# Output projection scalings dealt over the second product, weight tiles swapped, stores of combined down weights two steps later

## The chip, the cores and the metric

The kernel runs on one core of one Trainium2 chip. The core's engines are TensorE (PE, with its weight loads shown as PEld), VectorE (DVE), ScalarE (ACT), GpSimd (POOL) and SyncE (SP), which here issues the DMAs. The metric is device time in microseconds, the median of several executions.

## The reference

One decoder layer over 2048 rows of width 1024, all in float32. The parts that matter here are these:

```python
o_hg = rmsnorm(o_hg, hg_out_norm) * silu(hg)             # (T, 512)
o_sb = rmsnorm(stick_breaking_mix(sq, sk, sv), sb_out_norm)   # (T, 512)
mix = jnp.concatenate([o_hg, o_sb], axis=-1) @ w_out     # output projection
h = h + rmsnorm(mix, attn_post_norm)
u = rmsnorm(h, ffn_pre_norm)
gate, up = jnp.split(u @ w_gate_up, [D_FF], axis=-1)     # D_FF = 2816
y = (silu(gate) * up) @ w_down
h = h + rmsnorm(y, ffn_post_norm)
h = h + (p @ ple_proj) * sigmoid(h @ ple_gate)
```

## The kernel before

**Products.** The 2048 rows are worked on in four groups of 512. A float32 matrix product is made of three matmuls, from operands that are split into a high and a low half (`mm3`, L221 to L223). ACT casts the high half; DVE or POOL subtracts it from the source, which gives the low half (L207/L208, L845/L846 and L1073/L1074 in the profile). In the tile names `uh`/`ul` and `wh`/`wl` are such halves.

From group 2 on, two groups are taken together, and each pair of 2x2 block matrices is multiplied in seven products instead of eight, in the order `CHAIN = (1, 2, 6, 3, 7, 5, 4)`. The operands of some products are sums and differences of blocks (L1086, L1089); the results are added into `cu`, `c11`, `c12` and so on as each product ends (`chain`, also L1086/L1089).

**The joint output projection.** `out_pair(2)` projects groups 2 and 3. Position `pos` is 0 to 6, `prod` its product. Each product has four tiles `i` of twelve matmuls: four blocks `k`, three matmuls each. `w_prep(pos, k)` brings the weights: they come from `w_out` as `wr` and are split, or come from `wo_p` already split. `a_prep` brings the left operand. While tiles 0 and 1 of a position run, the weights of the next position are prepared, two blocks at each.

The left operand has a half that belongs to the stick-breaking group (`raws[4..7]`, in tiles named `wl` and `wh`), whose rows must be scaled by a factor that is not known earlier. `over_rows` spreads the factor over a tile (four transposes at L792 and a copy by ACT to `acc`, L794). `scaled` multiplies by it and by the gain `g_sb` (L798). The scaled blocks are then added to `s2`, and the sums are split as the left operand of product 6. All of this is written ahead of the last tile (i = 3) of product 1. Beside the products run the rest of the previous groups' work (`post_mix`, L930 to L955) and the first operands of gate_up.

**The down weights.** In the first gate_up (`gate_up(0)`, 77 steps, a step being one product of a block, two tiles), hooks run after given steps. At steps 36, 40, ... 76, `down_combos(k)` loads four blocks of `w_down` into `wr` buffers (`load`, L1058), combines them on DVE (`b_combos`, L1086) and stores the four results to `wd_s[k]` (L1104), which `down` reads later. Other hooks in these steps read rows of `h_s`, scale them on ACT (L992), transpose them on TensorE (`turner`: tile `hg`, L1006) and store them to `u_s` (L1012). The 12 `wr` buffers of that pool (`WR = 12`) also carry the weights of gate_up.

**Order.** TensorE's order is the written one. The order on DVE, ACT, POOL and SP comes from a simulation of the program's time; instructions under `pin` keep the written order among themselves.

Of the kernel before, what the change touches and what calls it, by code (L numbers as in the profile page):

```python
# [13 lines left out]
ALU = mybir.AluOpType  # L14

P = 128
# [3 lines left out]
GT = 512  # L20
NG = T // GT
TT = GT // P
HH = 4
SBH = 8
SBD = 64
DFF = 2816
# [64 lines left out]
def hybrid_block(  # L91
# [6 lines left out]
    nc = tc.nc  # L98
    ctx.enter_context(tc.manual_schedule(engines={mybir.EngineType.PE}))
    x, p, out = x[0], p[0, 0], out[0]  # L100
    w_in, w_out, w_gate_up, w_down = w_in[0], w_out[0], w_gate_up[0], w_down[0]
# [67 lines left out]
    def bank(tag):  # L169
        return ps.tile([P, 512], F32, tag=tag, name=tag, bufs=BANKS[tag])  # L170
# [4 lines left out]
    def mm_bank():  # L175
        mm_count[0] += 1
        return bank(mm_tags[mm_count[0] % len(mm_tags)])
# [25 lines left out]
    pin = tc.keep_in_program_order  # L203
# [21 lines left out]
    def cut(pair, j):  # L225
        return pair[0][:, j * P:(j + 1) * P], pair[1][:, j * P:(j + 1) * P]
# [58 lines left out]
    def operand(pool, tag, bufs):  # L285
        return [pool.tile([P, GT], F32R, tag=tag + s, name=tag + s, bufs=bufs) for s in ("h", "l")]
# [502 lines left out]
    def over_rows(rr, tag, new):  # L789
        b = bank(tag)  # L790
        for t in range(TT):
            nc.tensor.transpose(b[:, t * P:(t + 1) * P], rr[:, t:t + 1].to_broadcast((P, P)), ident)  # L792
        e = new()
        nc.scalar.copy(e, b)  # L794
        return e

    def scaled(k, raw, r):
        nc.vector.scalar_tensor_tensor(raw, raw, g_sb[:, k:k + 1], r, op0=ALU.mult, op1=ALU.mult)  # L798

    def first_rows(g, tt):  # L800
        acc = ev(name="oss")
# [21 lines left out]
    def out_pair(g, tt, rr):  # L823
        sw = {}
        cs = [{} for _ in range(TT)]
        raws, s2 = {}, {}

        def w_prep(pos, k):
            prod = CHAIN[pos]
            if pos % 2:  # L830
                hi, lo = slot("wh", 0, "wh", F32R), slot("wl", 0, "wl", F32R)
            else:
                hi, lo = operand(wpool, "u", UB)
            sw[prod, k] = hi, lo
            if prod in (6, 3, 7):
                for n, t in enumerate((hi, lo)):
                    nc.sync.dma_start(t.bitcast(F32), wo_p[k][KEPT[prod], n])
                return
            raw = wpool.tile([P, GT], F32, tag="wr", name="wr", bufs=4)
            if prod in (1, 2):  # L840
                r = (HH * (prod - 1) + k) * P
                nc.sync.dma_start(raw, w_out[r:r + P, 0:GT])
            else:
                nc.sync.dma_start(raw, wo_s[k][0 if prod == 5 else 1])
            nc.scalar.copy(hi, raw)  # L845
            (V if k % 2 else G).tensor_tensor(lo, raw, hi.bitcast(F32), op=ALU.subtract)  # L846

        def a_prep(pos, k):
            prod = CHAIN[pos]
            if prod == 3:  # L850
                a12 = load(on_s[k])
                sub(V, s2[k], a12, s2[k])
                t, e = s2[k], V
            elif prod == 7:
                t = load(o_s[g][k])
                sub(V, t, t, raws[k])
                e = V
            elif prod == 5:
                t = raws[k]
                add(V, t, t, raws[HH + k])  # L860
                e = V
            else:
                t, e = raws[HH + k], V
            tt[prod, k] = split(wpool, "u", UB, t, e)

        def rows(half, j, i):
            m = cs[i][1 + half, 1 + j]
            nc.sync.dma_start(h2_s[g + half][i * P:(i + 1) * P, j * GT:(j + 1) * GT], m)
            nc.scalar.activation(junk, m, AF.Square, scale=ROOT, accum_out=sums_m[half][:, 2 * i + j:2 * i + j + 1])

        def before(pos, i):
            if (pos, i) == (0, 3):
                r = over_rows(rr, "tr", new_acc)
                for k in range(HH):
                    scaled(k, raws[HH + k], r)
                    add(V, s2[k], s2[k], raws[HH + k])
                    tt[6, k] = split(wpool, "u", UB, s2[k], V)

        def new_acc():
            return slot("acc", 0, "acc")  # L880

        for k in range(HH):
            w_prep(0, k)
        for i in range(ND):
            if i in (2, 3):
                raws[i] = slot("wr", 0, "wr")
            else:
                tag = "wh" if i % 2 else "wl"
                raws[i] = wpool.tile([P, GT], F32, tag=tag, name=tag, bufs=3)
            nc.sync.dma_start(raws[i], o_s[g + 1][i])  # L890
        for k in range(HH):
            s2[k] = load(o_s[g][k])
            sub(V, s2[k], raws[k], s2[k])
        for k in range(HH):
            w_prep(1, k)
        for pos, prod in enumerate(CHAIN):
            for i in range(TT):
                before(pos, i)
                b = mm_bank()
                for k in range(HH):  # L900
                    mm3(b, cut(tt[prod, k], i), sw[prod, k], k == 0, k == HH - 1)
                chain(prod, cs[i], b, new_dn)
                if prod == 2:
                    rows(0, 0, i)
                elif prod == 5:
                    rows(0, 1, i)
                    rows(1, 1, i)
                elif prod == 4:
                    rows(1, 0, i)
                if 1 <= pos < len(CHAIN) - 1 and i < 2:  # L910
                    for k in (2 * i, 2 * i + 1):
                        w_prep(pos + 1, k)
                        if pos > 1:
                            a_prep(pos + 1, k)
                yield
            if prod in (5, 4):
                half = 0 if prod == 5 else 1
                r, x = row_scales[:, half, 0:TT], hgss[:, g + half, :]
                pair = sums_m[half].rearrange("p (t j) -> p t j", j=2)
                nc.gpsimd.tensor_tensor(r, pair[:, :, 0], pair[:, :, 1], op=ALU.add)  # L920
                for _ in range(2):
                    nc.gpsimd.tensor_tensor(r, r, x, op=ALU.mult)
                nc.gpsimd.tensor_scalar(r, r, EPS, None, op0=ALU.add)
                nc.gpsimd.tensor_tensor(r, r, neghalf.to_broadcast((P, TT)), op=ALU.pow)
                nc.gpsimd.tensor_tensor(r, r, x, op=ALU.mult)
# [126 lines left out]
    def slot(tag, side, name, dt=F32):  # L1052
        side = side if big[side] is not None else 0
        return big[side].tile([P, GT], dt, tag=f"{tag}{side}", name=name, bufs=SLOTS[tag.rstrip("hl")][side])

    def load(src, shape=None):
        r = slot("wr", 0, "wr")
        nc.sync.dma_start(r if shape is None else shape(r), src)  # L1058
        return r
# [25 lines left out]
    def sub(e, o, a, b):  # L1085
        return e.tensor_tensor(o, a, b, op=ALU.subtract)  # L1086

    def add(e, o, a, b):
        return e.tensor_tensor(o, a, b, op=ALU.add)  # L1089

    V, G = nc.vector, nc.gpsimd

    def b_combos(b11, b12, b21, b22, e):

        sub(e, b11, b12, b11)
        sub(e, b12, b22, b12)
        sub(e, b22, b22, b11)
        sub(e, b21, b22, b21)

    def combos(blk, dst, e):  # L1100
        t = [load(blk(i, j)) for i, j in ((0, 0), (0, 1), (1, 0), (1, 1))]
        b_combos(*t, e)
        for i, r in zip((1, 3, 4, 2), t):
            nc.sync.dma_start(dst[i - 1], r)  # L1104

    wd_s = [dram.tile([4, P, GT], F32, tag=f"wd_s{k}", name=f"wd_s{k}") for k in range(DFF // 256)]
    wp_s = [dram.tile([4, P, GT], F32, tag=f"wp_s{k}", name=f"wp_s{k}") for k in range(ND // 2)]

    def down_combos(k):
        def blk(i, j):  # L1110
            r = (2 * k + i) * P
            return w_down[r:r + P, j * GT:(j + 1) * GT]

        combos(blk, wd_s[k], V)

    def ple_combos(k):
        def blk(i, j):
# [354 lines left out]
    g_sb = column("g_sb", sb_out_norm[0], HH, later)  # L1472
# [121 lines left out]
    def at(stage, step, f):  # L1594
        hooks.setdefault((stage, step), []).append(f)

    def spread(stage, step, gen, n, every=1):
        st = Stream(gen)
        for i in range(n):
            at(stage, step + i * every, st.step)  # L1600
# [4 lines left out]
    def turner(src, dst, gain, scales=None):  # L1605
        return turn(src, dst, gain, ["hg"], wr, acc, scales)
# [4 lines left out]
    spread(0, 19, post_late(NG - 1), 2 * TT, 4)  # L1611
    for k in range(DFF // 256):
        at(0, 36 + 4 * k, lambda k=k: down_combos(k))
    spread(0, 34, turner(h_s[2], u_s[2], g_ffn, rows_h[0]), 10, 2)
    spread(0, 54, turner(h_s[3], u_s[3], g_ffn, rows_h[1]), 10, 2)
    spread(2, 59, make_pt(), 9, 2)
# [42 lines left out]
```

## Time and profile before

| | |
|---|---|
| median of 3 runs | 2965.28 us (2963.56 to 2966.44) |
| the profiled execution | 2966.78 us, its span 2965.0 us, granted clock 0.992 |
| TensorE busy | 97% of the span, 17796 matmuls |
| DVE / ACT / POOL busy | 71% / 53% / 47% |
| DMA | 635.27 MB, queue 1 busy 67.5% of 16 engines' span |

In rows of the profile a line names time and duration (us), engine, source line, operation, `output<-input` and the tile's shape. In brackets stands how long the engine was idle before it, and what released it. Rows `SPq` are DMA issues. A wait in a list is given as engine, tile and line, who released it, then the sum in us, how often, and the longest.

### The profile page before, as it was taken

How to read it: one execution, taken by the hardware profiler on the slowest of the kernel's cores; microseconds unless marked ns; L12 is line 12 of the kernel's file. 1: busy time of each engine (PE TensorE's matmuls, PEld its weight loads, DVE VectorE, ACT ScalarE, POOL GpSimd, SP SyncE). 2: the span in 40 equal slices, each digit the busy share in tenths (PEclk: the TensorE clock that was granted, in tenths of full speed). 3: DMA queues.
4: the chain of work that ended last, by engine and by line, in shares of the span. 5: the costliest groups of instructions: out<-in, count | busy, mean ns of one | idle time of the engine just before them, and what ended most of it. 6: DMA issues, size and time to landing. Idle time of an engine off the chain costs nothing. (4 is left out here: it accounts for less than half of the span.)

```text
span 2965.0 us, 51986 instructions
## 1 busy us (share of the span) xinstructions
PE 2862.4 (97%) x17796; PEld 2397.8 (81%) x17796; DVE 2114.2 (71%) x3051; ACT 1581.2 (53%) x3220; POOL 1387.7 (47%) x1384
## 2 busy tenths in 40 slices
PE   9999999999999999988999999999999999999999
PEld 7878888877888788877788778788888888888777
DVE  4776777777788777756977777756877765666685
ACT  5667657666667666765623333455433233545542
POOL 3345456545665666764433211355722121456653
PEclk9999999999999999999999999999999999999999
DMA  7785576456556454448986787867965555677975
GB/s 230 234 257 169 173 222 207 143 168 211 182 184 183 147 155 131 142 146 310 331 283 211 253 275 265 269 204 226 325 217 174 177 172 174 214 221 236 329 253 168
DMA packets 487561, 635.27 MB, mean 214 GB/s; under 512 B 45184, under 2 KB 275584, under 8 KB 487296
## 3 DMA queue, kind: packets, MB, share of 16 engines
q1 hardware_dynamic: 487296, 631.95, 67.5%
q8 instruction: 141, 2.31, 0.3%
q14 instruction: 124, 1.02, 0.1%
HBM read 459.29 MB, written 172.49 MB: 213 GB/s over the span
## 5 line engine op out<-in xcount | busy, mean ns | idle before, releaser
L1073 ACT CAST wh<-wr 128x512 fp32r<-128x512 f32 x592 | 347.1, 618 | 501.0 <-PE mm L222 110.5
L1074 POOL TENSOR_TENSOR wl<-wr,wh 128x512 fp32r<-128x512 f32 x256 | 370.2, 1454 | 439.8 <-ACT wh L1073 390.6
L452 POOL TENSOR_TENSOR a<-be,ring 128x512 f32<-128x512 f32 (+2 forms) x320 | 325.5, 1018 | 410.0 <-DVE ring L448 382.9
L1074 DVE TENSOR_TENSOR wl<-wr,wh 128x512 fp32r<-128x512 f32 x336 | 303.4, 911 | 159.4 <-ACT wh L1073 136.4
L221 PE MATMUL mm<-uh,wh 128*128 128x512 f32 x968 | 401.4, 415 | 7.9 <-DVE vv L365 4.4
L223 PE MATMUL mm<-uh,wl 128*128 128x512 f32 x968 | 380.5, 393 | 0.0
L222 PE MATMUL mm<-ul,wh 128*128 128x512 f32 x968 | 380.2, 393 | 0.0
L448 DVE TENSOR_TENSOR_SCAN ring<-z,ring,be 128x512 f32<-128x512 f32 x192 | 245.6, 1279 | 88.2 <-ACT z L434 83.5
L221 PE MATMUL mm<-wh,uh 128*128 128x256 f32 (+1 forms) x840 | 262.4, 312 | 2.9 <-DVE eb L351 2.2
L222 PE MATMUL mm<-wl,uh 128*128 128x256 f32 (+1 forms) x840 | 249.4, 297 | 4.1 <-POOL wl L208 2.6
L223 PE MATMUL mm<-wh,ul 128*128 128x256 f32 (+1 forms) x840 | 248.7, 296 | 0.0
L433 ACT ACTIVATE be<-z 128x512 f32<-128x512 f32 (+2 forms) x320 | 171.1, 535 | 100.6 <-DVE z L431 60.9
L465 DVE TENSOR_TENSOR al<-tr,ah 128x512 fp32r<-128x512 f32 (+1 forms) x320 | 191.6, 599 | 43.7 <-ACT ah L463 42.1
L221 PEld LDWEIGHTS mm<-uh,wh 128*128 128x128 f32 x968 | 183.5, 190 | 43.4 <-issue 3.8
L223 PEld LDWEIGHTS mm<-uh,wl 128*128 128x128 f32 x968 | 182.5, 189 | 41.2
L207 ACT CAST wh<-wr 128x512 fp32r<-128x512 f32 x256 | 158.6, 619 | 102.4 <-PE mm L222 51.1
L463 ACT CAST ah<-tr 128x512 fp32r<-128x512 f32 (+1 forms) x320 | 167.8, 524 | 84.6 <-PE tr L460 83.0
L208 POOL TENSOR_TENSOR wl<-wr,wh 128x512 fp32r<-128x512 f32 x128 | 171.5, 1340 | 78.8 <-ACT wh L207 58.7
L222 PEld LDWEIGHTS mm<-ul,wh 128*128 128x128 f32 x968 | 183.4, 190 | 30.4
L460 PE MATMUL tr<-ident,a 128*128 128x128 f32 x1088 | 178.4, 276 | 19.5 <-POOL a L452 19.5
L427 PE MATMUL z<-kt,q 128*128 128x512 f32 (+3 forms) x640 | 189.4, 377 | 0.0
L1074 POOL TENSOR_TENSOR wl<-s,wh 128x512 fp32r<-128x512 f32 x40 | 62.2, 1557 | 269.8 <-ACT wh L1073 224.9
(387 smaller groups left out, 7598.3 us busy)
## 6 DMA issues: line engine op xcount, KB each, us to landing
wr<-in_w_gate_up_dram SPq DMA_DIRECT2D x292, 256.0 KB, 4.3
wr<-in_w_in_dram SPq DMA_DIRECT2D x224, 256.0 KB, 3.3
wr<-hid_s SPq DMA_DIRECT2D x154, 256.0 KB, 3.1
wr<-in_w_down_dram SPq DMA_DIRECT2D x110, 256.0 KB, 3.6
wr<-h_s SPq DMA_DIRECT2D x96, 256.0 KB, 4.5
wr<-wd_s SPq DMA_DIRECT2D x88, 256.0 KB, 3.1
kt<-k_s SPq DMA_DIRECT2D x80, 256.0 KB, 3.2
vt<-v_s SPq DMA_DIRECT2D x80, 256.0 KB, 3.3
```

Of the source, the lines that this page charges most:

```text
L208: (lo_engine or nc.gpsimd).tensor_tensor(lo, src, hi.bitcast(F32), op=ALU.subtract)
L221: nc.tensor.matmul(o, l[0], r[0], start=start, stop=False)
L222: nc.tensor.matmul(o, l[0], r[1], start=False, stop=False)
L223: nc.tensor.matmul(o, l[1], r[0], start=False, stop=stop)
L427: nc.tensor.matmul(z[:, :n], st["q"][i][:, tb * P:(tb + 1) * P], ch["k"][:, :n], start=i == 0, stop=i == 1)
L433: nc.scalar.activation(be[:, :n], z[:, :n], AF.Sigmoid, scale=0.125)
L448: nc.vector.tensor_tensor_scan(r[:, o:o + n][:, ::-1], z[:, :n][:, ::-1], be[:, :n][:, ::-1], init, op0=ALU.mult, op1=ALU.bypass)
L452: nc.gpsimd.tensor_tensor(a[:, :n], be[:, :n], r[:, o + 1:o + n + 1], op=ALU.mult)
L460: nc.tensor.transpose(tr[:, tb * P:(tb + 1) * P], ch["a"][tb][:, sb * P:(sb + 1) * P], ident)
L465: nc.vector.tensor_tensor(lo[:, lo_c:], tr[:, lo_c:], hi[:, lo_c:].bitcast(F32), op=ALU.subtract)
L1073: nc.scalar.copy(hi, src)
L1074: lo_engine.tensor_tensor(lo, src, hi.bitcast(F32), op=ALU.subtract)
```

## The change

Three parts, in the diff:

```diff
     def scaled(k, raw, r):
-        nc.vector.scalar_tensor_tensor(raw, raw, g_sb[:, k:k + 1], r, op0=ALU.mult, op1=ALU.mult)
+        return nc.vector.scalar_tensor_tensor(raw, raw, g_sb[:, k:k + 1], r, op0=ALU.mult, op1=ALU.mult)
...
         def w_prep(pos, k):
             prod = CHAIN[pos]
-            if pos % 2:
+            if pos % 2 == 0:
                 hi, lo = slot("wh", 0, "wh", F32R), slot("wl", 0, "wl", F32R)
             else:
                 hi, lo = operand(wpool, "u", UB)
...
         def before(pos, i):
             if (pos, i) == (0, 3):
-                r = over_rows(rr, "tr", new_acc)
-                for k in range(HH):
-                    scaled(k, raws[HH + k], r)
+                raws["r"] = over_rows(rr, "tr", new_acc)
+            if pos == 1:
+                for k in ((0,), (1, 2), (3,), ())[i]:
+                    pin(scaled(k, raws[HH + k], raws["r"]))
                     add(V, s2[k], s2[k], raws[HH + k])
                     tt[6, k] = split(wpool, "u", UB, s2[k], V)
...
+    down_parts = {}
+
     def down_combos(k):
-        def blk(i, j):
-            r = (2 * k + i) * P
-            return w_down[r:r + P, j * GT:(j + 1) * GT]
-
-        combos(blk, wd_s[k], V)
+        r = 2 * k * P
+        down_parts[k] = t = [
+            load(w_down[r + i * P:r + (i + 1) * P, j * GT:(j + 1) * GT]) for i, j in ((0, 0), (0, 1), (1, 0), (1, 1))]
+        b_combos(*t, V)
+
+    def down_store(k):
+        for i, r in zip((1, 3, 4, 2), down_parts.pop(k)):
+            pin(nc.sync.dma_start(wd_s[k][i - 1], r))
...
         at(0, 36 + 4 * k, lambda k=k: down_combos(k))
+        at(0, min(38 + 4 * k, 7 * DFF // 256 - 1), lambda k=k: down_store(k))
```

The row factor is still spread ahead of tile 3 of product 1. The scalings, with the additions and splits that follow each, are written ahead of the tiles of product 2: block 0 ahead of tile 0, blocks 1 and 2 ahead of tile 1, block 3 ahead of tile 2; the scalings are pinned. The weights of the even positions (products 1, 6, 7, 4) now lie in the four `wh`/`wl` slots of the right-hand pool, those of the odd ones (2, 3, 5) in the tiles named `u`. The four stores of a round of down weights are issued two steps after its loads (pinned; in the last round in the same step). In the changed file most lines behind the first edits stand one lower, the stores at L1120 instead of L1104.

**DVE, between products 1 and 2.** L798 are the scalings, L1089 (L1090 after) additions, L846 low halves of weights, L1074 (L1075) and L208 splits of operands, L938/L939 (L939/L940) rows of `post_mix`, `c_...` evictions of product 2's tiles. Before:

```order
1465 L798 SCALAR_TENSOR_TENSOR wl<-wl,g_sb,acc 128x512
1466 L798 SCALAR_TENSOR_TENSOR wh<-wh,g_sb,acc 128x512
1467 L798 SCALAR_TENSOR_TENSOR wl<-wl,g_sb,acc 128x512
1468 L798 SCALAR_TENSOR_TENSOR wh<-wh,g_sb,acc 128x512
1469 L1089 TENSOR_TENSOR wr<-wr,wl 128x512
1470 L1089 TENSOR_TENSOR wr<-wr,wh 128x512
1471 L1089 TENSOR_TENSOR wr<-wr,wl 128x512
1472 L938 SCALAR_TENSOR_TENSOR mix<-mix,rstd_18700,gb 128x512 x2
1473 L1089 TENSOR_TENSOR wr<-wr,wh 128x512
1474 L1074 TENSOR_TENSOR ul<-wr,uh 128x512
1475 L846 TENSOR_TENSOR wl<-wr,wh 128x512
```

After, the same place:

```order
1460 L846 TENSOR_TENSOR ul<-wr,uh 128x512
1461 L939 SCALAR_TENSOR_TENSOR mix<-mix,rstd_18613,gb 128x512
1462 L940 TENSOR_TENSOR h<-h,mix 128x512
1463 L846 TENSOR_TENSOR ul<-wr,uh 128x512
1464 L939 SCALAR_TENSOR_TENSOR mix<-mix,rstd_18676,gb 128x512 x2
1465 L940 TENSOR_TENSOR h<-h,mix 128x512
1466 L798 SCALAR_TENSOR_TENSOR wl<-wl,g_sb,acc 128x512
1467 L1090 TENSOR_TENSOR wr<-wr,wl 128x512
1468 L208 TENSOR_TENSOR ul<-wr,uh 128x512
1469 L1090 TENSOR_TENSOR c_18712<-av,cu 128x512
1470 L798 SCALAR_TENSOR_TENSOR wh<-wh,g_sb,acc 128x512
```

Both of product 2's low halves on DVE (L846, now in `ul`) stand ahead of the first scaling, where before the last of them stood behind all four; the second scaling stands behind the eviction of product 2's first tile.

**DVE, at the end of product 2.** `c_18806` and `c_18823` are the evictions of its third and fourth tile. Before:

```order
1480 L1089 TENSOR_TENSOR c_18730<-av,cu 128x512
1481 L1086 TENSOR_TENSOR wr<-wr 128x512 x4
1482 L1089 TENSOR_TENSOR c_18755<-mm,cu 128x512
1483 L208 TENSOR_TENSOR ul<-wr,uh 128x512 x2
1484 L1089 TENSOR_TENSOR c_18806<-z,cu 128x512
1485 L208 TENSOR_TENSOR ul<-wr,uh 128x512 x2
1486 L1089 TENSOR_TENSOR c_18823<-mm,cu 128x512
```

After:

```order
1480 L939 SCALAR_TENSOR_TENSOR mix<-mix,rstd_18770,gb 128x512 x2
1481 L798 SCALAR_TENSOR_TENSOR wh<-wh,g_sb,acc 128x512
1482 L208 TENSOR_TENSOR ul<-wr,uh 128x512
1483 L1090 TENSOR_TENSOR c_18806<-z,cu 128x512
1484 L1090 TENSOR_TENSOR c_18823<-mm,cu 128x512
1485 L1090 TENSOR_TENSOR wr<-wr,wh 128x512
1486 L1087 TENSOR_TENSOR wr<-wr 128x512
1487 L940 TENSOR_TENSOR h<-h,mix 128x512
1488 L208 TENSOR_TENSOR ul<-wr,uh 128x512 x2
```

The fourth scaling now stands directly ahead of these evictions, behind a row of `post_mix` that needs a factor from POOL (`rstd`), and its addition (1485) and split (the first of 1488) behind them.

**SP, around the second round of down weights.** `u_s<-acc` is a turner's store, `h_s<-wr` a store of rows. Before:

```order
1163 L1058 DMA wr<-in_w_down_dram 128x512 x2
1164 L1104 DMA wd_s_232<-wr 128x512
1165 L1058 DMA wr<-in_w_down_dram 128x512 x2
1166 L1104 DMA wd_s_232<-wr 128x512 x2
1167 L1058 DMA wr<-in_w_gate_up_dram 128x2x256
1168 L1104 DMA wd_s_232<-wr 128x512
1169 L1058 DMA wr<-in_w_gate_up_dram 128x2x256
1170 L1012 DMA u_s_101<-acc 128x512
1171 L1058 DMA wr<-in_w_gate_up_dram 128x2x256 x6
```

After:

```order
1161 L1059 DMA wr<-in_w_down_dram 128x512 x4
1162 L1059 DMA wr<-in_w_gate_up_dram 128x2x256
1163 L1013 DMA u_s_101<-acc 128x512
1164 L1059 DMA wr<-in_w_gate_up_dram 128x2x256 x5
1165 L1013 DMA u_s_101<-acc 128x512
1166 L1059 DMA wr<-in_w_gate_up_dram 128x2x256 x2
1167 L1120 DMA wd_s_232<-wr 128x512 x4
```

The stores stood between the loads of down weights and gate_up weights; now they stand behind eight loads of gate_up weights.

## The prediction

> **What bounds the kernel now.** I read the page first, then TensorE's stalls in the two stretches that the change touches, then the rows around each stall on the engine that ends it. The last two lines here are stretches of time: their length, busy time of PE, PEld, DVE, ACT and POOL, then the granted clock.
>
> ```profile
> span 2965.0 us, 51986 instructions
> PE 2862.4 (97%) x17796; PEld 2397.8 (81%) x17796; DVE 2114.2 (71%) x3051; ACT 1581.2 (53%) x3220; POOL 1387.7 (47%) x1384
> 1362.30:1382.00 19.70, 13.92 (x49) 10.82 (x48) 16.81 (x27) 10.82 (x24) 8.14 (x5) 0.83 0.71 247
> 1661.00:1761.00 100.00, 93.43 (x410) 75.70 (x409) 71.91 (x103) 37.40 (x72) 24.43 (x19) 0.97 0.79 267
> ```
>
> TensorE is busy 97% of the span, so all its idle time is 2965.0 − 2862.4 = 102.6 us, and the change leaves its list of instructions alone but for tile names. What can be won is idle time, and matmuls at a lowered clock behind it, which the page counts as busy. The windows show two such places: the second product of the joint output projection (clock 0.83), and 100 us inside the first gate_up. Within them:
>
> ```profile
> PE av L222 <- DVE wl L846: 5.8, 1, 5.8
> PE hg L1006 <- ACT wr L992: 6.5, 2, 3.5
> 1347.20 0.40 PE L221 MATMUL mm<-uh 128*128 128x512 f32 x1
> 1351.47 0.50 PE L222 MATMUL mm<-ul,uh 128*128 128x512 f32 x1 [1.49 <-DVE ul L846]
> 1352.54 0.63 PE L223 MATMUL z<-uh,ul 128*128 128x512 f32 x1
> 1355.92 0.40 PE L222 MATMUL z<-ul,uh 128*128 128x512 f32 x1
> 1356.38 0.39 PE L221 MATMUL mm<-uh 128*128 128x512 f32 x1
> 1359.11 0.60 PE L792 MATMUL tr<-ident,rq 128*128 128x128 f32 x4
> 1362.31 0.39 PE L221 MATMUL av<-wh,uh 128*128 128x512 f32 x1
> 1370.68 0.79 PE L222 MATMUL av<-wl,uh 128*128 128x512 f32 x1 [5.78 <-DVE wl L846]
> 1382.05 0.39 PE L221 MATMUL z<-uh 128*128 128x512 f32 x1
> ```
>
> The tile from 1356.38 to 1359.11 is undisturbed: twelve matmuls in 2.73 us. Four of them make a product, 10.92. Product 1 runs from 1347.20 to 1362.31, product 2 from there to 1382.05.
>
> **The scalings.** Why product 2 waited shows on DVE:
>
> ```profile
> 1361.03 0.75 DVE L798 SCALAR_TENSOR_TENSOR wl<-wl,g_sb,acc 128x512 f32<-128x512 f32 x1 [6.71 <-ACT acc L794]
> 1363.02 0.74 DVE L798 SCALAR_TENSOR_TENSOR wh<-wh,g_sb,acc 128x512 f32<-128x512 f32 x1
> 1369.95 0.68 DVE L846 TENSOR_TENSOR wl<-wr,wh 128x512 fp32r<-128x512 f32 x1
> ```
>
> DVE stood 6.71 us for the row factor, then did all four scalings and four additions before the low half of product 2's last weight block. In the new order that half stands ahead of the first scaling, with other work of product 1. Product 2 then takes 10.92 instead of 19.74: 8.8 won. Product 1's own stall and slow second tile go too, because the loads of its weights and its subtractions now come earlier: 15.11 − 10.92 − 0.60 (the transposes) = 3.6 won.
>
> What is late next: the scalings themselves. Their results are product 6's left operand, due when product 2 ends. The fourth scaling is now behind the third and behind two POOL-fed rows of post_mix, and the last addition stands behind the evictions of product 2's last two tiles. From the last eviction on DVE has five operations up to the low half of block k=3 (eviction, add, sub, h add, split), at the pitch of 0.66 us that the four scalings show (1361.03 to 1363.02 is three pitches): 3.3 us. TensorE can cover nine matmuls of 0.23 (2.73/12), 2.0 us, so 1.3 of stall at least. If the POOL-fed rows are late as well, it is up to the 5.8 that this change removes. I take the middle, 3.3.
>
> A stall is also followed by a lower clock: matmuls of 0.63 instead of 0.40 us from 1352.54 to 1355.92, after an idle of only 1.49. The two tiles from 1347.20 to 1356.38 took 9.18 where 5.46 would do; beside the 1.49 idle that leaves 2.2 for the clock. Between nothing and 2.2 I add 1.2: 4.5 lost at product 6, ends 1.3 and 8.0. The Trainium skill ("TensorE: Matmul & The Clock Gate", Part 1, What's actually happening) has the clock halved after an idle window of about 3.4 us and restored after as much busy time. The trace agrees with the second (3.4 us slow) and not with the first, since 1.49 us sufficed; by the page's rule the 3.3 us stall would cost no clock and the total would come out 1.2 us lower, and I follow the trace.
>
> **The swapped weight tiles.** Products 1, 6, 7 and 4 now use the four slots of the right-hand pool, the odd ones the tiles named u. With four blocks per product and four slots, product 6's loads wait for product 1's last tile, product 7's for product 6's, and so on. No transfer is added. Two effects can be priced.
>
> ```profile
> 1341.59 1.26 POOL L208 TENSOR_TENSOR wl<-wr,wh 128x512 fp32r<-128x512 f32 x1
> 1342.81 1.28 POOL L846 TENSOR_TENSOR ul<-wr,uh 128x512 fp32r<-128x512 f32 x1
> 1342.90 0.39 PE L222 MATMUL mm<-wl,uh 128*128 128x256 f32 x1 [2.14 <-POOL wl L208]
> 1406.71 0.48 PE L221 MATMUL z<-uh 128*128 128x512 f32 x1
> 1413.45 0.50 PE L223 MATMUL z<-uh,ul 128*128 128x512 f32 x1 [2.72 <-DVE ul L208]
> 1415.84 0.63 PE L221 MATMUL mm<-uh 128*128 128x512 f32 x1
> 1419.29 0.60 PE L949 MATMUL tr<-ident,mix 128*128 128x128 f32 x4
> ```
>
> First, at the end of the projection of group 1, TensorE waits for POOL's last weight half. In the new POOL order two subtractions of product 1's weights (1.28 each) stand ahead of it. One can partly fall into an earlier wait of POOL, so 1.3 to 2.6: I take 1.8 lost.
>
> Second, product 7. Its first two tiles take 12.58 where 5.46 would do: 7.1 lost, since its left operand, loaded again from o_s, comes late. In the new SP order these loads follow product 7's weights, which only wait for the end of product 6, one product (10.92) ahead of product 7. What is left is DVE: from the last eviction of product 3 on there are four operations to block k=2 and three more to k=3, 0.2 + 7 × 0.66 = 4.8 us, against 2.3 that TensorE covers, some 2.4 of stall and 0.8 of clock. So 3.9 won, ends 0 (nothing changes) and 7.1.
>
> Third, gate_up's first weights share these slots' release: 0.5 lost, ends 0 and 2. The row factor is held through most of product 2 in one of two buffers; the next claim on them is 34 steps into gate_up, so that costs nothing.
>
> Sum here: 1.8 − 3.6 − 8.8 + 4.5 − 3.9 + 0.5 = −9.5.
>
> **The stores two steps later.** 44 stores, the same bytes; only their place in SP's queue moves. A pinned store that waits holds up the gate_up loads behind it, but the subtractions it needs then have two steps:
>
> ```profile
> wr<-in_w_down_dram SPq DMA_DIRECT2D x110, 256.0 KB, 3.6
> ```
>
> A step is one product of a block, two tiles, 5.46 us; so 10.9 us stand against 3.6 of landing and four DVE operations. The two stalls in gate_up are transposes of rows that ACT must first scale:
>
> ```profile
> 1672.33 0.60 PE L1006 MATMUL hg<-ident,wr 128*128 128x128 f32 x4
> 1686.86 1.67 PE L1006 MATMUL hg<-ident,wr 128*128 128x128 f32 x4 [3.00 <-ACT wr L992]
> 1700.20 0.60 PE L1006 MATMUL hg<-ident,wr 128*128 128x128 f32 x4
> 1722.92 0.60 PE L1006 MATMUL hg<-ident,wr 128*128 128x128 f32 x4
> 1737.94 1.67 PE L1006 MATMUL hg<-ident,wr 128*128 128x128 f32 x4 [3.49 <-ACT wr L992]
> 1751.32 0.60 PE L1006 MATMUL hg<-ident,wr 128*128 128x128 f32 x4
> 1665.87 0.33 SPq L1104 DMA_DIRECT2D wd_s<-wr  x1
> 1671.34 1.05 SPq L1104 DMA_DIRECT2D wd_s<-wr  x2
> 1674.61 3.53 SPq L1058 DMA_DIRECT2D wr<-in_w_gate_up_dram  x6
> 1681.42 0.69 DVE L1089 TENSOR_TENSOR s<-wr 128x512 f32<-128x512 f32 x1 [5.61 <-DMA wr<-in_w_gate_up_dram]
> 1684.68 0.62 ACT L1073 CAST wh<-wr 128x512 fp32r<-128x512 f32 x1 [17.20 <-DVE wr L1086]
> 1710.37 8.62 SPq L1058 DMA_DIRECT2D wr<-in_w_gate_up_dram  x4
> 1719.55 3.78 SPq L1058 DMA_DIRECT2D wr<-in_w_gate_up_dram  x2
> ```
>
> Their normal spacing is 22.72/2 = 11.36 (1700.20 to 1722.92). The first stall makes it 14.53 and, through the clock, the next 13.34: 3.17 + 1.98 = 5.15 lost. The second 15.02 and 13.38: 3.66 + 2.02 = 5.68. In the first, SP waits at the stores of the combinations for DVE (1665.87, 1671.34); the six gate_up loads behind them go out from 1674.61; DVE waits 5.61 us for them at 1681.42; ACT's cast waits 17.2 for DVE, and the scaling of the rows is queued behind that cast. In the new order the loads stand ahead of the stores, DVE's evictions ahead of the sums over these weights, and the rows' scaling ahead of that cast. I take the whole 5.15.
>
> The second is less sure: SP was held at 1710.37 for buffers, 8.62 us for four loads, and two more waited for the store of h. The new order moves that store behind all six, and one cast fewer stands ahead of the scaling, but the buffers are if anything scarcer. Ends −5.7 (gone) and +1; I take 60%, 3.4. What waits behind a delayed load is the same chain, so the price if the cover goes is another 5.4 per stall. Sum here −8.5.
>
> **Total.** −9.5 − 8.5 = −18 against the profiled execution's 2966.78 gives 2948.8. That execution is 1.5 above the median of the three, 2965.28, so I forecast 2947.
>
> **The rivals.** *Starved buffers (slower).* The loads share 12 buffers, and four are now held two steps longer (10.9 us) in each round of four steps. SP waits on this already:
>
> ```profile
> SPq L1058 <- DMA wd_s<-wr: 9.5, 12, 2.5
> ```
>
> That is under 1 us a time, which speaks against; the 8.62 at 1710.37 speaks for. If the old two stalls stay and five more rounds of the eleven get one of 5.4, −9.5 + 27 = +17.5: 2983. From three new ones on, −9.5 + 16 = +6.7, it is slower by over 0.2% (5.9 us, about what a measurement of this kernel tells from no change). *The stall only moves*: product 6 waits as much as product 2 did, 8.8 instead of 4.5: −13.7, 2952 (to 2954 if product 7 gains less). The POOL-fed row ahead of the last scaling is for it; that the scalings now begin while DVE stood idle for 6.71 us is against. *The late stores do nothing*: the transposes wait for other things, only −9.5 is left, 2956. The second stall's blame on buffers speaks for it, the first's rows against. *Both of these*: −5.2, 2960, no change to be told.
>
> **How the numbers follow.** Forecast 0.42 (2939 to 2951 by the ends of its terms); stall moves 0.17; stores do nothing 0.18; both 0.11; starved 0.09; 0.03 for a new stall at gate_up's start that eats most. Faster: 0.42 + 0.17 + 0.17 = 0.76. Same 0.13, slower 0.11. The range 2939 to 2962 leaves out the starved case and the far ends.
>
> **What will show it.** Product 2 in 11 us with no wait on DVE wl at its first tile; a wait of 1 to 5 us on DVE at product 6's first tile; the POOL wait ahead of product 1 near 4; product 7's first two tiles near 8.6; transposes 11.36 apart through gate_up. New SP waits on wd_s stores of several us, or TensorE waiting for gate_up's weights, would prove the forecast wrong; so would a wait at product 6 over 7.

## The result and the profile after

The changed kernel takes 2955.62 us (median of six runs, 2948.17 to 2957.18), the kernel before, run beside it, 2967.84: a ratio of 0.9954 (95% interval 0.9941 to 0.9966), which is 13.6 us faster (10.1 to 17.5); the two medians themselves are 12.2 apart. The profiled execution took 2955.99, 10.8 less than that of before. The forecast was −18.

The page after: span and busy times, then the two stretches of the prediction (length, busy PE, PEld, DVE, ACT, POOL, granted clock, DMA share, GB/s), the first now being product 2 alone.

```profile
span 2954.2 us, 51949 instructions
PE 2856.8 (97%) x17796; PEld 2394.6 (81%) x17796; DVE 2115.3 (72%) x3051; ACT 1580.9 (54%) x3220; POOL 1404.1 (48%) x1384
1363.20:1374.10 10.90, 10.90 (x49) 9.01 (x48) 10.03 (x15) 8.15 (x20) 2.71 (x4) 1.00 0.92 349
1661.00:1761.00 100.00, 97.29 (x433) 79.31 (x432) 79.34 (x118) 35.60 (x68) 29.52 (x15) 0.98 0.86 286
```

TensorE is idle for 97.4 us instead of 102.6. The other half of the gain is in its busy time (2856.8 against 2862.4, the same 17796 matmuls): fewer of them run at the lowered clock. Product 2 runs without a break, at clock 1.00 instead of 0.83. TensorE's waits for the operands of products 6 and 7, from the list of its waits, 1300 to 1500 us:

```profile
PE z L223 <- DVE ul L208: 3.5, 2, 2.6
PE z L221 <- ACT uh L207: 2.3, 2, 1.7
```

The wait on the weights' low half (`wl` L846, 5.8) is not in that list any more. The rows of the projection, TensorE after:

```profile
1331.18 0.28 PE L623 MATMUL tr<-ones,acc 128*128 128x1 f32 x2
1344.89 0.58 PE L222 MATMUL mm<-wl,uh 128*128 128x256 f32 x1 [5.13 <-POOL wl L208]
1350.82 0.35 PE L222 MATMUL mm<-wl,uh 128*128 128x256 f32 x1
1351.84 0.40 PE L221 MATMUL mm<-wh,uh 128*128 128x512 f32 x1
1363.23 0.39 PE L221 MATMUL av<-uh 128*128 128x512 f32 x1
1374.11 0.39 PE L221 MATMUL z<-wh,uh 128*128 128x512 f32 x1
1378.68 0.80 PE L223 MATMUL z<-wh,ul 128*128 128x512 f32 x1 [2.60 <-DVE ul L208]
1381.13 0.80 PE L221 MATMUL z<-wh,uh 128*128 128x512 f32 x1 [1.65 <-ACT uh L207]
1392.92 0.48 PE L221 MATMUL mm<-uh 128*128 128x512 f32 x1
1405.59 0.48 PE L221 MATMUL z<-wh,uh 128*128 128x512 f32 x1
1419.87 0.39 PE L221 MATMUL mm<-uh 128*128 128x512 f32 x1
1441.63 0.39 PE L221 MATMUL tr<-uh,wh 128*128 128x512 f32 x1
```

The wait on POOL ahead of product 1, once 2.14, is 5.13 (1344.89), and 2.60 + 1.65 of the waits above fall into product 6. The rows that carry no wait here, but for 1350.82, are the first ones of the stretches that the tables below use. The attention ahead does not end at the same time in every trace: the first transpose of `ones`, just ahead of group 1's last product tiles, begins at 1331.18 here, at 1332.00 before, and anywhere from 1324.82 to 1335.03 in the fourteen traces. So a stretch is timed from that transpose. *Tail* is from there to product 1 (1351.84), then come the products in their order, and *to hg* is from gate_up's first matmul (1441.63) to the last of the group of transposes in the next fence (1739.69).

```profile
1666.34 0.60 PE L1007 MATMUL hg<-ident,wr 128*128 128x128 f32 x4
1677.70 0.60 PE L1007 MATMUL hg<-ident,wr 128*128 128x128 f32 x4
...
1726.33 1.67 PE L1007 MATMUL hg<-ident,wr 128*128 128x128 f32 x4 [2.47 <-ACT wr L993]
1739.69 0.60 PE L1007 MATMUL hg<-ident,wr 128*128 128x128 f32 x4
```

The first stall of 3.00 is gone (1666.34 to 1677.70 is the undisturbed 11.36); the spacing behind it is 11.90. The second is 2.47 instead of 3.49, with slow matmuls behind it as before.

| us | tail | product 1 | 2 | 6 | 3 | 7 | 5 and 4 | to hg |
|---|---|---|---|---|---|---|---|---|
| before | 15.20 | 15.11 | 19.74 | 11.68 | 12.98 | 18.94 | 10.88 each | 303.91 |
| after | 20.66 | 11.39 | 10.88 | 18.81 | 12.67 | 14.28 | 10.88 each | 298.06 |
| difference | +5.5 | −3.7 | −8.9 | +7.1 | −0.3 | −4.7 | 0 | −5.9 |

These add up to −10.8, which is the difference of the spans; the ends outside cancel (−0.8 and +0.8).

### The profile page after: what moved, and what is told of

It reads as the page before. It is cut to its first block, busy times and chain, and to the rows that moved or that the text cites. A ratio compares the mean times of both kernels' runs of the same rounds, so it can differ in the third digit from the quotient of the medians.

```text
span 2954.2 us, 51949 instructions
## 1 busy us (share of the span) xinstructions
PE 2856.8 (97%) x17796; PEld 2394.6 (81%) x17796; DVE 2115.3 (72%) x3051; ACT 1580.9 (54%) x3220; POOL 1404.1 (48%) x1384
## 5 line engine op out<-in xcount | busy, mean ns | idle before, releaser
L1074 ACT CAST wh<-wr 128x512 fp32r<-128x512 f32 x592 | 346.9, 619 | 489.0 <-PE mm L222 103.5
L1075 POOL TENSOR_TENSOR wl<-wr,wh 128x512 fp32r<-128x512 f32 x256 | 366.6, 1439 | 437.3 <-ACT wh L1074 395.2
L1075 DVE TENSOR_TENSOR wl<-wr,wh 128x512 fp32r<-128x512 f32 x336 | 296.4, 890 | 175.1 <-ACT wh L1074 153.8
L1075 POOL TENSOR_TENSOR wl<-s,wh 128x512 fp32r<-128x512 f32 x40 | 85.6, 2146 | 271.6 <-ACT wh L1074 242.8
L208 POOL TENSOR_TENSOR wl<-wr,wh 128x512 fp32r<-128x512 f32 x128 | 172.4, 1347 | 81.4 <-ACT wh L207 59.9
```

Of the source, the lines that this page charges most:

```text
L208: (lo_engine or nc.gpsimd).tensor_tensor(lo, src, hi.bitcast(F32), op=ALU.subtract)
L1074: nc.scalar.copy(hi, src)
L1075: lo_engine.tensor_tensor(lo, src, hi.bitcast(F32), op=ALU.subtract)
```

## The experiments

**What was to be told apart.** The theory, as in the prediction: dealing the scalings frees product 2, and its other side is the new wait at product 6; the swap only costs at the tail and gains at product 7; the late stores remove gate_up's stalls. The rival: the swap frees product 2, by bringing its weights' subtractions earlier, and the dealing is not needed. Ratios are against the kernel before on the same chip.

### The late stores alone

```diff
+        at(0, min(38 + 4 * k, 7 * DFF // 256 - 1), lambda k=k: down_store(k))
```

(with `down_combos` and `down_store` as in the change, nothing else of it)

> Only the down stores are moved two steps later. Theory A (the parts add up): the stretch of the output projection stays as before, the first gate_up stall goes and about 1 us of the second, so the time falls by 5.9 us (5 to 7). Rival B (the gate_up stalls went because the output projection ended 5.8 us sooner and shifted everything): nothing changes, within 2 us.

Measured: 2956.48, ratio 0.9965 (0.9952 to 0.9978), −10.4 us. TensorE at the transposes that had the first stall, and at those that had the second:

```profile
1683.32 0.60 PE L1006 MATMUL hg<-ident,wr 128*128 128x128 f32 x4
1729.45 1.52 PE L1006 MATMUL hg<-ident,wr 128*128 128x128 f32 x4 [0.50 <-ACT wr L992]
```

Both stalls are gone but for 0.50, and the stretch *to hg* is 10.6 shorter (293.31). That is more than the 5 to 7 expected ahead of this run; the −8.5 of the prediction lies within the interval (−6.5 to −14.2). SP's queue shows that the mechanism is the one named there; in 1600 to 1880 us, before and after:

```profile
SPq L1104 <- DVE wr L1086: 47.1, 28, 4.9
```

```profile
SPq L1120 <- DVE wr L1087: 13.3, 11, 3.7
SPq L1059 <- DVE wl L1075: 42.6, 24, 7.5
SPq L1059 <- DMA wd_s<-wr: 10.8, 11, 2.5
```

SP stood 47.1 us at the stores, now 13.3 (13.8 with the stores alone). DVE's wait for gate_up's weights ahead of the first stall, 5.61 before, is 1.82 after (at 1675.91). The wait on the stores' landing went from 9.5 to 10.8 only. What did grow is SP's wait at the loads for DVE to free a buffer, from 24.0 to 42.6 (44.5 with the stores alone): the buffers are scarcer, as the rival had it, but TensorE hardly waits: the loads go out early enough.

### The scalings alone, the swap alone, and both

```diff
-                r = over_rows(rr, "tr", new_acc)
-                for k in range(HH):
-                    scaled(k, raws[HH + k], r)
+                raws["r"] = over_rows(rr, "tr", new_acc)
+            if pos == 1:
+                for k in ((0,), (1, 2), (3,), ())[i]:
+                    pin(scaled(k, raws[HH + k], raws["r"]))
```

> Only the scalings are dealt; weight tiles as before. Theory A (the swap is what brings product 2's last weight half ahead of the scalings): that half still stands behind a POOL-fed row and the first scaling on DVE, product 2's first tile still waits 4 to 6 us, and the time changes by 0 to -4 us. Rival B (dealing alone frees DVE): product 2 loses its wait, product 6 waits some 2 us, and the time falls by 6 to 9 us.

```diff
-            if pos % 2:
+            if pos % 2 == 0:
                 hi, lo = slot("wh", 0, "wh", F32R), slot("wl", 0, "wl", F32R)
```

> Only the weight tiles are swapped; the four scalings stay together ahead of product 1's last tile. Theory A: product 2's wait goes as in the full change, product 6 does not wait because all scalings are done some 8 us before it starts, POOL's wait ahead of product 1 is 5 us as in the full change; the time falls by 12 us (9 to 14), more than with the dealing added. Rival B (the dealing is needed): product 2 still waits 4 us or more and the time falls by 4 us at most.

And the two together, without the stores:

> Dealt scalings and swapped tiles, stores as before. If the parts add up: gate_up begins 5.8 us sooner than before, both gate_up stalls are as before (3.0 and 3.5 us), the time falls by 5.8 us (4 to 7). If the parts interact: the gate_up stalls shrink or go as well, and the time falls by 9 us or more.

Measured: the scalings alone 1.0005 (0.9994 to 1.0016), +1.5 us; the swap alone 0.9973 (0.9962 to 0.9985), −8.0; both 0.9997 (0.9985 to 1.0009), −0.9. Here the theory fell, at product 2. TensorE with the scalings alone:

```profile
1365.12 0.50 PE L222 MATMUL av<-wl,uh 128*128 128x512 f32 x1 [3.41 <-DVE wl L846]
1380.41 0.77 PE L221 MATMUL z<-uh 128*128 128x512 f32 x1 [3.43 <-DMA uh<-wo_p]
```

With the swap alone:

```profile
1344.96 0.58 PE L222 MATMUL mm<-wl,uh 128*128 128x256 f32 x1 [5.74 <-POOL wl L208]
1363.17 0.39 PE L221 MATMUL av<-uh 128*128 128x512 f32 x1
1374.05 0.39 PE L221 MATMUL z<-wh,uh 128*128 128x512 f32 x1
```

Dealing alone leaves product 2 waiting 3.41 us on the very half that it waited for before, and product 6 then waits as long for weights that were loaded late. The swap alone takes product 2 from 1363.17 to 1374.05, 10.88 with no wait, though all four scalings are still written together ahead of product 1's last tile. Why shows in the queues. ACT's cast of product 2's last weight block before, then, with the swap alone, DVE's last subtraction for product 2 and its first scaling:

```profile
1363.72 0.63 ACT L845 CAST wh<-wr 128x512 fp32r<-128x512 f32 x1
```

```profile
1355.86 1.46 DVE L846 TENSOR_TENSOR ul<-wr,uh 128x512 fp32r<-128x512 f32 x1 [0.24 <-ACT uh L845]
1363.17 1.78 DVE L798 SCALAR_TENSOR_TENSOR wl<-wl,g_sb,acc 128x512 f32<-128x512 f32 x1
```

Before, that weight was cast only after product 2 had begun (1362.31); in the tiles of the swap its cast is at 1355.21, and the low half follows 7 us ahead of the first scaling. The swap also brings the POOL wait at the tail. Product 6, whose operand is then ready, takes 11.68. Still, the −8.0 falls short of the 9 to 14 expected of the swap: products 3 and 7 take 33.31 us in this run, 26.95 in the full change.

| us | tail | product 1 | 2 | 6 | 3 | 7 | seven products |
|---|---|---|---|---|---|---|---|
| scalings | 14.60 | 15.1 | 16.33 | 18.72 | 12.67 | 16.73 | 101.31 |
| swap | 20.55 | 11.39 | 10.88 | 11.68 | 14.19 | 19.12 | 89.02 |
| both | 19.37 | 11.39 | 10.88 | 17.84 | 12.66 | 15.47 | 90.00 |

So what the dealing gains at products 3 and 7 (5 us) it loses at product 6 (6). Both together came out at no gain, which neither expectation had, although the seven products are 10.2 us shorter than before and the tail 4.2 longer. The loss stands elsewhere, at the start of the down product. TensorE and POOL, scalings and swap together:

```profile
1897.37 0.79 PE L222 MATMUL z<-wl,wh 128*128 128x512 f32 x1 [8.21 <-POOL wl L1075]
1888.68 8.64 POOL L1075 TENSOR_TENSOR wl<-wr,wh 128x512 fp32r<-128x512 f32 x1 [4.47 <-ACT wh L1074]
1888.68 12.35 POOL L1075 TENSOR_TENSOR wl<-wr,wh 128x512 fp32r<-128x512 f32 x4 [4.47 <-ACT wh L1074]
```

The first of four subtractions on POOL took 8.64 us of their 12.35, and TensorE stood 8.21 for it; the other kernels wait 1 to 2 us at most at one time there. From the last of the transposes (*to hg*) to its end this execution is 10.7 us longer than before. (Its span is 3.1 shorter all the same, since its `ones` began 7.2 earlier and the stretch from there to product 5 is 6.0 shorter.) No edit touches that place, and why this kernel alone has it there was not followed up.

### The swap and the late stores, without the dealing

```diff
-            if pos % 2:
+            if pos % 2 == 0:
...
+        at(0, min(38 + 4 * k, 7 * DFF // 256 - 1), lambda k=k: down_store(k))
```

> Swapped tiles and late stores, scalings together as before. If the parts add up: product 6 does not wait, both gate_up stalls are gone as with the stores alone, and the time falls by 18 us (15 to 20). Rival (an earlier begin of gate_up brings the second gate_up stall back, as the full change shows): that stall stays at 2 to 3 us and the time falls by 11 to 14 us.

Measured: 2951.82, ratio 0.9955 (0.9942 to 0.9967), −13.3 us, the same as the full change's −13.6. With the late stores, the dealing contributes nothing that can be measured (each gain is known to some 3.7 us either way); without them the swap alone was 7 us better than both (0.9973 against 0.9997, two intervals that just touch). The gain also falls short of the sum of the two parts, −10.4 and −8.0, which the intervals alone would not exclude. The trace shows where: the projection (tail 19.71, products 88.42) keeps what the swap gave, but the stretch *to hg* is 297.6 instead of 293.3, for the second stall is back. TensorE:

```profile
1721.79 1.66 PE L1006 MATMUL hg<-ident,wr 128*128 128x128 f32 x4 [3.05 <-ACT wr L992]
```

The stores alone left 0.50 of it, with the swap it is 3.05, in the full change 2.47. What brings it back was not found. That the projection ends earlier is not enough: in the last run below gate_up begins at 1441.42, as in the full change (1441.63), and TensorE has no such stall.

### The POOL wait at the tail

The subtractions of product 1's weights all go to DVE, in the full change and in the kernel without the dealing:

```diff
-                (V if k % 2 else G).tensor_tensor(lo, raw, hi.bitcast(F32), op=ALU.subtract)
+                (V if k % 2 or pos == 0 else G).tensor_tensor(lo, raw, hi.bitcast(F32), op=ALU.subtract)
```

> The full change, with product 1's low weight halves all on DVE, so that POOL's order ahead of product 1 is free of them. Theory A (POOL's order makes the wait of 5.13 us ahead of product 1): the wait shrinks to 2 us or less and the slowed matmuls behind it go, 4 to 6 us better than the full change, so 17 to 19 us better than before; product 6 still waits. Rival B (the late cast or load of the last weight makes it): the wait stays above 4 us and the time is that of the full change.

> Swapped tiles, late stores, scalings together as before, product 1's low weight halves on DVE. If all three causes add up: no wait above 2.5 us ahead of product 1, none at products 2 and 6, gate_up as with the stores alone: 22 us better than before (18 to 25). If the gains of the projection are given back in gate_up: 13 to 17 us.

Measured: 0.9961 (0.9946 to 0.9975), −11.6 us, and 0.9958 (0.9941 to 0.9974), −12.5; no better than without the edit. The wait did shrink. TensorE with the edit in the full change, where product 6 begins at 1370.41:

```profile
1341.07 0.39 PE L222 MATMUL mm<-wl,uh 128*128 128x256 f32 x1 [2.68 <-POOL wl L208]
1370.41 0.50 PE L221 MATMUL z<-wh,uh 128*128 128x512 f32 x1 [1.13 <-ACT uh L207]
1380.96 0.79 PE L221 MATMUL z<-wh,uh 128*128 128x512 f32 x1 [3.71 <-ACT uh L207]
1393.52 0.48 PE L221 MATMUL mm<-uh 128*128 128x512 f32 x1
```

5.13 became 2.68 and the tail 16.65 instead of 20.66. So the two subtractions ahead of POOL's last one were the cause of most of what that wait had grown by (it was 2.14 before). But product 6 took 23.11 instead of 18.81, product 2 12.17 and product 7 15.69 instead of 10.88 and 14.28: 4.0 won, 7.0 lost. In the kernel without the dealing the tail won 1.6 (18.08), and products 3 and 7 took 16.5 and 21.07 instead of 14.19 and 18.51, 4.9 lost.

### Whether rows fed by POOL pace the projection

DVE's queue holds four rows of `post_mix` that wait for a factor from POOL, one directly ahead of the last scaling. First, the scalings are dealt so that all are written ahead of tile 1 of product 2:

```diff
-                for k in ((0,), (1, 2), (3,), ())[i]:
+                for k in ((0, 1), (2, 3), (), ())[i]:
```

> The full change with scalings of blocks 0 and 1 ahead of tile 0 and of 2 and 3 ahead of tile 1, so that the last one stands ahead of the row of post_mix that needs POOL's factor. Theory A (that row holds the last scaling): product 6 takes 11.7 to 13.5 us instead of 18.8; products 3 and 7 may take up to 5 us of it back, as in the run with the swap alone. Against before 15 to 19 us better. Rival B (the evictions, or the additions, hold it): product 6 still takes 17 us or more and nothing changes against the full change.

Measured: 0.9954 (0.994 to 0.9967), −13.6 us. The last scaling now stands ahead of the row (at 1373.22, the row at 1376.62), yet product 6 takes 17.09, only 1.7 less: that row is not the main thing that holds it. Then group 1's `post_mix` is rewritten so that DVE needs no factor: POOL multiplies by it and adds the row, in the full change, without the dealing, and without the dealing but with the edit on the tail:

```diff
-                nc.vector.scalar_tensor_tensor(d, d, r, gb[j], op0=ALU.mult, op1=ALU.mult)
-                (nc.gpsimd if j else nc.vector).tensor_tensor(hs[j], hs[j], d, op=ALU.add)
+                if g == 1:
+                    nc.vector.tensor_tensor(d, d, gb[j], op=ALU.mult)
+                    nc.gpsimd.tensor_scalar(d, d, r, None, op0=ALU.mult)
...
+                (nc.gpsimd if j or g == 1 else nc.vector).tensor_tensor(hs[j], hs[j], d, op=ALU.add)
```

> The full change, and post_mix of group 1 computed so that no DVE instruction waits for POOL's factor: DVE multiplies by the gain ahead of the factor, POOL multiplies by the factor and adds. Theory A (POOL-fed rows in DVE's queue pace the projection, and what one product wins the next gives back): DVE has no wait on the factor any more (6.5 us in the full change), product 6 takes 11.7 to 13 us instead of 18.8, and the time is 5 to 8 us below the full change, 18 to 22 below before. Rival B (it is the sheer work on DVE and ACT, or late loads): product 6 stays above 16 us, or another product takes up what it wins, and the time is within 3 us of the full change.

> Swapped tiles and late stores with scalings together, and the same post_mix. Theory A: products 3 and 7, which take 14.2 and 18.5 us there, fall to 12.7 and 12 to 14, since DVE's waits on the factor (8.2 us) stood ahead of product 7's subtractions; 5 to 7 us below the run with swap and stores, 18 to 22 below before. Rival B: the two products stay within 2 us of that, and so does the time.

> As the run before it, with product 1's low weight halves on DVE too. Theory A: with DVE free of waits, the 3 to 4 us won ahead of product 1 are kept: 22 to 26 us below before. Rival B: they are lost again at products 3 and 7 as without the new post_mix, and the time is that of the run before it or worse.

Measured: 0.9975 (0.9965 to 0.9986), −7.4 us; 0.9964 (0.995 to 0.9979), −10.7; 0.9976 (0.9966 to 0.9986), −7.1. All of them gain less than the full change in their middle values. Without the dealing product 3 falls to 12.66, as hoped, but product 7 rises to 22.27; with the edit on the tail as well, the tail is 16.56 and products 6, 3 and 7 take 18.13, 14.88 and 20.74. DVE's waits from product 1 to product 5, full change, and then with `post_mix` rewritten:

```profile
DVE mix L939 <- POOL rstd L276: 6.5, 4, 4.1
```

```profile
DVE mix L940 <- ACT junk L271: 9.6, 3, 6.0
```

The wait on POOL is gone, and DVE waits 9.6 us for ACT in its place, in the multiplication that was to be free. Product 6 takes 20.87. That test is therefore no clean one. The last takes the factor itself away: the rows of group 1 use a constant.

```diff
+            r = row_rstd(gb if g == 1 else mix[t])
+            r = neghalf if g == 1 else r
```

(in both places of `post_mix` where a factor is made)

> The full change with post_mix of group 1 cut loose from its own row factors: the squares, sums and powers are still computed by ACT and POOL, but of a tile that is ready, and the rows are multiplied by a constant instead, so this part of the output is not normalised; the instructions stay, the serial wait goes. Theory A (the chain of post_mix, square, factor, rows, square, factor, paces the projection by holding DVE's or ACT's queue): product 6 takes 11.7 to 13 us instead of 18.8 and products 3 and 7 no more than 12.7 and 14.3, so the projection is 6 to 9 us shorter, and the time 5 to 9 us below the full change. Rival B (the work on DVE and the loads pace it, whoever waits): the seven products together stay within 3 us of 89.8 us, and the time within 3 us of the full change.

Measured: 0.9967 (0.9953 to 0.9982), −9.8 us. TensorE at the starts of products 6 and 3:

```profile
1373.09 0.39 PE L221 MATMUL z<-wh,uh 128*128 128x512 f32 x1
1388.90 0.48 PE L221 MATMUL mm<-uh 128*128 128x512 f32 x1
```

Product 6 takes 15.81 instead of 18.81, product 7 18.09 instead of 14.28, and the seven products 90.60 instead of 89.79. The idea that these rows pace the projection fell. What this kernel gains in its trace on the full change, 4.6 us of span, lies behind the projection: its *to hg* is 292.74 instead of 298.06.

**What the runs have in common.** From the first transpose of `ones` to product 5 it is 86.4 (swap and stores) to 92.6 (the last kernel with `post_mix` on POOL) in the eleven kernels that have the swap (before 93.6, the stores alone 93.0, the scalings alone 94.2). None of the edits tried on top of the swap made it shorter than the swap and the stores do. This stretch before, after, and with swap and stores (columns as above):

```profile
1332.00:1425.60 93.60, 78.76 (x378) 64.20 (x377) 65.27 (x95) 57.32 (x138) 37.54 (x35) 0.93 0.86 295
```

```profile
1331.20:1419.90 88.70, 77.24 (x379) 64.31 (x378) 65.67 (x92) 55.38 (x135) 31.65 (x33) 0.92 0.89 308
```

```profile
1329.70:1416.10 86.40, 76.67 (x379) 63.84 (x378) 67.57 (x94) 55.10 (x135) 34.52 (x33) 0.92 0.92 319
```

Each moves 27.3 to 27.6 MB (295 GB/s over 93.60 us, 308 over 88.70, 319 over 86.40), with the DMA engines busy for 86 to 92% of it. Transfers that are nearly always under way would explain why a wait taken away comes back at another product. It is argued from these three lines, not shown: no run changed the bytes, and which transfer is late when stays open. DVE's work, the same in all three (65.3 to 67.6 us busy), is a rival that no run took away either.

## Why the prediction was right, and where it was not

The direction, the range (2939 to 2962) and the removal of most of the named stalls came true: 2955.62. The forecast of 2947 was 8.6 too low. Of that, 2.6 is the kernel before, whose six runs now give 2967.84 where the three gave 2965.28. The rest is a gain of −13.6 (−12.2 by the medians) instead of −18. In the profiled pair it is −10.8, and the difference of 7 us has its terms:

| term | forecast | trace |
|---|---|---|
| POOL wait ahead of product 1 | +1.8 (1.3 to 2.6) | +5.5 |
| product 1 | −3.6 | −3.7 |
| product 2 | −8.8 | −8.9 |
| product 6 | +4.5 (1.3 to 8.0) | +7.1 |
| products 3 and 7 | −3.9 (−7.1 to 0) | −5.0 |
| gate_up's first weights | +0.5 (0 to 2) | 0 |
| first stall in gate_up | −5.15 | −4.6 |
| second stall | −3.4 (−5.7 to +1) | −1.1 |

Added up and counted from 2965.28, the ends of these terms reach from 2937.5 to 2961.3, not from 2939 to 2951 as the prediction has it for the forecast alone; the range that it states comes to nearly the same.

**Product 2: right in size, wrong in cause.** The step "in the new order that half stands ahead of the first scaling" is what the order shows, but it was put down to the dealing. The swap alone makes product 2 10.88, the dealing alone leaves a wait of 3.41. Product 1's gain was put down to the dealing, too, and is the swap's (11.39 with the swap alone, 15.1 with the dealing alone). The order of the whole change does not tell which of its edits put a row where it is. That both sizes came out within 0.1 us is in part luck: the two edits were changed together, so it did not matter which of them did it.

**The POOL wait: the term that left its bounds.** The step "two subtractions of product 1's weights (1.28 each) stand ahead of it" was right in kind, as the edit at the tail shows. Two things were missing. POOL, the last subtraction among them:

```profile
1341.91 1.26 POOL L846 TENSOR_TENSOR wl<-wr,wh 128x512 fp32r<-128x512 f32 x1
1343.13 1.70 POOL L208 TENSOR_TENSOR wl<-wr,wh 128x512 fp32r<-128x512 f32 x1
```

The two ahead took 1.60 and 1.26, and the last one itself 1.70 where it had 1.26 before (a POOL subtraction of this shape at 1338.24 took 1.68 before, so the rows of before had both sizes). And behind the idle of 5.13 comes a lowered clock that the term did not hold, though product 6's did. TensorE after, the clock is the third number from the end:

```profile
1344.80:1350.80 6.00, 5.91 (x27) 5.91 (x28) 3.27 (x7) 2.10 (x5) 2.37 (x5) 0.50 1.05 375
```

The wait grew by 3.0, and from its end to product 1 it is 6.95 us instead of 4.30 (before, 1342.90 to 1347.20), another 2.65.

**Product 6.** The chain named (fourth scaling behind a row that needs POOL's factor, behind evictions) is there. DVE after, with the last scaling's neighbours:

```profile
1374.89 1.41 DVE L939 SCALAR_TENSOR_TENSOR mix<-mix,rstd,gb 128x512 f32<-128x512 f32 x2 [0.85 <-POOL rstd L276]
1376.22 0.74 DVE L798 SCALAR_TENSOR_TENSOR wh<-wh,g_sb,acc 128x512 f32<-128x512 f32 x1
```

The last scaling began at 1376.22, 2.1 after product 2 had ended (1374.11). The 3.3 us taken for the wait became 2.60 + 1.65, and the clock behind it cost more than the 1.2: without a wait this product takes 11.68 (before, and with the swap alone), and 18.81 − 11.68 − 4.25 = 2.9. The row itself is the smaller part of the chain: with the last scaling ahead of it, product 6 still takes 17.09. The sum lies between the forecast and the rival of the moved stall (8.8), whose total of −13.7 is the one that came; the miss at the tail and at the second stall brought it there, not product 6 alone.

**The other rivals.** Late stores that do nothing: excluded, alone they give −10.4. Starved buffers: SP's queue shows them, TensorE does not. Product 7 gained 4.7 where 3.9 was forecast, but the runs show it as the dealing's return for product 6, not as the swap's: with the swap alone product 7 takes 19.12. The second stall was rightly called the less sure one, and in the traces it is what keeps the change from the sum of its two useful parts.

**The clock.** It was halved behind an idle of 5.13 and of 2.60, and still so behind the 1.65 that followed. By the Trainium skill ("TensorE: Matmul & The Clock Gate", Part 1, What's actually happening) only an idle window of about 3.4 us would do that; the trace agrees for the first and not for the second. The prediction took from one stall that 1.49 us suffice. The same trace speaks against so plain a rule, for behind the 2.14 idle ahead of product 1 the kernel before went on at the full clock:

```profile
1343.13 0.28 PE L223 MATMUL mm<-wh,ul 128*128 128x256 f32 x1
```

(The same matmul took 0.41 behind the 5.13 in the kernel after.) Of these idles of 1.49, 2.14 and 2.60 the middle one left the clock as it was, so their length alone does not tell.

## What to carry to other kernels

Where several edits reorder the same queues, the printed order shows what moved and not which edit moved it: run each alone, since here the edit that gave its place in the order no gain (the dealing) stood beside the one that did (the swap). In the projection here, where transfers were under way for 86 to 92% of the time, waits that were removed came back at another product; count from a fixed point ahead of a wait to a fixed point behind it before calling its removal a gain. Price a delay on a queue with the clock behind the stall, which here cost half to two thirds of the stall again (2.65 behind 5.13, 2.9 behind 4.25).

## What was not expected of the hardware

Two short idles in a row (2.60 and 1.65 us) kept TensorE at half clock. The last stretch, after:

```profile
1378.60:1385.00 6.40, 4.66 (x9) 2.94 (x10) 6.16 (x12) 4.38 (x11) 1.24 (x2) 0.50 0.76 195
```

Between them it ran a single matmul; this one and those behind it took 0.63 to 0.80 instead of 0.39, to 1385.01. After the idle of 5.13 the halved clock lasted 5.9 us (1344.89 to 1350.82), as it had lasted 5.7 before behind the idle of 5.78 (1370.68 to 1376.37), but 3.4 behind the idle of 1.49. And a POOL subtraction of 128x512, 1.26 to 1.7 in the rows above, took 8.64 at 1888.68. The stretch around it, scalings and swap together:

```profile
1888.30:1901.00 12.70, 4.13 (x10) 3.04 (x11) 7.90 (x14) 6.22 (x12) 12.32 (x4) 0.65 0.47 156
```

DVE's 7.90 us are without a gap and end at 1896.20. POOL's first subtraction ends 1.1 behind that, at 1897.32, and the three that follow beside an idle DVE take 1.27 each. So it looks as if POOL had to wait for a pause of DVE. The Trainium skill ("SBUF — State Buffer", SBUF: two separate sides) says that DVE, in an operation with two inputs in SBUF, and GpSimd lock each other out for the whole of an instruction. These rows agree with that, but go further: POOL got no turn between a dozen instructions of DVE. Elsewhere it did: in the full change one subtraction took 7.11 (at 1725.37, TensorE did not wait for it) and ended while DVE went on without a gap, and the two at the tail took 1.26 and 1.70. The longest in the kernel before took 3.26. No run separated the lock from another cause.
